# Rows of 320 columns and a chosen byte place for the streamed operands of an encoder's large products

## The chip, the core and the metric

The kernel runs on one core of one Trainium2 chip. The metric is the device time of one execution in microseconds (us). The kernel before takes 2589.96 us, the median of three runs (2589.75 to 2590.74).

A core has a matrix engine (TensorE, PE in the profile), a vector engine (DVE), a scalar engine (ACT), GpSimd (POOL) and a queue engine (SP), which work on a shared on-chip memory (SBUF) of 128 partitions. A matmul multiplies a stationary operand, which a weight load (PEld) brings into the engine, by a streamed operand, whose columns are read one after another from SBUF. The sums land in PSUM.

## What is computed

The reference is a two-layer encoder on 256 tokens with 16 learned tokens ahead of them, 272 positions in all, of width 2048, in float32. Of each layer:

```python
h = rmsnorm(x)
q, k, v, f, ga, gf = split(h @ W_in)            # 2048 -> 6656
a = attention(rope(rmsnorm(q)), rope(rmsnorm(k)), v) @ W_attn_br
s = Re(fft2(f)) @ W_four                        # over positions and 128 channels
x = x + (sigmoid(ga) * a + sigmoid(gf) * s) @ W_out
u = rmsnorm(x) @ W_up                           # 2048 -> 2 * 5632
x = x + (silu(dwconv3(u_gate)) * u_val) @ W_down
```

The 16 learned tokens are dropped at the end, so layer 1 needs only the last 258 positions behind the keys, values and Fourier input, and the last 256 from the gated product on.

## The kernel before, in words

Activations stand transposed: 128 channels on the partitions, positions along the columns. Each float32 value is split in two parts of a rounded type, high and low, and a product takes three matmuls: high weights by high activations, high by low, low by high (lines 246, 247, 248 in `group`). Weights are stationary, 128 by 128 at a time; activations are streamed, 272 columns per matmul in layer 0, 258 or 256 in layer 1. Where twice the width fits 512 columns (layer 1's value half of `W_up` and `W_down`), the first two are one matmul over both parts of the activations (line 242, 512 columns: two rows of 256), followed by line 243 (256 columns).

Weights come as chunks of 512 KB (four contraction tiles by 256 output channels), 864 of them, in a fixed order, on SP's queue into `raw` (four buffers). ACT rounds each into `wh` (line 191), DVE subtracts into `wl` (line 194); `wh` and `wl` have three buffers each, and the split runs up to two chunks ahead of PE. `group` takes its chunks in order: for each contraction tile `kt` (four per chunk) and each of two output tiles `m`, three matmuls. In the last chunk of a group the order is `m` first, then `kt`. So in the other chunks six matmuls in a row read the rows of one `kt`, and in the last chunk three.

The streamed operands of the large products are:

- `xHL`, the normed activations, [16 tiles, high and low, 272 columns]: input projection, gates, `W_up` (groups f, k, v, q, ga, gf, ug, uv)
- `qH`, `qL`, the attention's output, 8 rows each: `W_attn_br` (group a)
- `mH`, `mL`, the gated sum, 8 rows each: `W_out` (group o, twice a layer)
- `gHL`, the feed-forward product, [24, high and low, 272]: `W_down` (group d)

Not among them are the Fourier branch's `fr` (group s, lines 281 and 282), the attention's own operands and the small helper products.

A row of 272 float32 columns is 1088 bytes, four times 256 and 64 more. Tiles stand in SBUF one after another in the order in which they are made. From their sizes follow these places in bytes: `xHL` 33,920; the six buffers of `wh` and `wl` 102,528 and on, each 4,096 long; the per-layer pool from 140,672, in it `mH` 149,376 and `mL` 162,432. Below, the phase of an operand is the place of the first element that a matmul reads, modulo 256. Every 128-column piece of `wh` and `wl` begins at phase 128. The rows of `xHL` begin at phases 128, 192, 0, 64 in turn (high, low, high, low), those of `mH` and of `mL` both at 128, 192, 0, 64 for successive `kt`, and `gHL`'s as `xHL`'s. In layer 1 the streamed part begins 14 columns (56 bytes) or 16 columns (64 bytes) into the row.

Of the kernel before, what the change touches and what calls it, by code (L numbers as in the profile page):

```python
# [10 lines left out]
F32 = mybir.dt.float32  # L11
F32R = mybir.dt.float32r
AF = mybir.ActivationFunctionType
ALU = mybir.AluOpType
# [10 lines left out]
NH = 8  # L25
# [8 lines left out]
MG = 2  # L34
FF_SPLIT = (24, 20)
PRE = 26

def _branch(text):
    return tuple((t[:-1], int(t[-1])) for t in text.split())
# [6 lines left out]
HC = 64  # L46
HC1 = HC + 1
TH = T // 2 + 2
BLK = ((0, 16), (16, 144), (144, 272))

C_COS, C_SIN, C_MASK = 0, T, 2 * T
# [58 lines left out]
def encoder_kernel(ctx, tc, xT, params, consts, bmat, w_in, w_abr, w_four, w_f64, w_out, w_up, w_down, outT):  # L110
# [179 lines left out]
    def first_groups(pss):  # L290
        assert order[st["grp"]][0] == (0, "f01")
        st["grp"] += 1
        ps = [psum.tile([P, 512], F32, tag="mm", name=f"ps_f01_{m}") for m in range(2 * MG)]
        pss += [ps[:MG], ps[MG:]]

        def tile_mm(j, k, h, lo):
            c = k % CW
            for m in range(MG):
                sl = slice(m * P, (m + 1) * P)
                o = ps[MG * j + m][:, :T]  # L300
                a, b = xH[:, k, :], xL[:, k, :]
                nc.tensor.matmul(o, h[:, c, sl], a, start=k == 0, stop=False)
                nc.tensor.matmul(o, h[:, c, sl], b, start=False, stop=False)
                nc.tensor.matmul(o, lo[:, c, sl], a, start=False, stop=k == KT - 1)

        for i, c0, c1, ks in ((0, 0, 1, (0,)), (0, 1, 2, (1,)), (1, 0, 2, ()), (0, 2, 4, (2, 3)), (1, 2, 4, ())):
            for k in ks:
                norm_split(k, P_NM)
            split_w(i, c0, c1, nc.vector if (i, c0) == (0, 0) else None)
        ws = [splits.pop(i) for i in range(2)]  # L310
        st["fetch"] = st["next"] = 2
        for n, (j, k) in enumerate((j, k) for k0 in (0, 2) for j in range(2) for k in (k0, k0 + 1)):
            tile_mm(j, k, *ws[j])
            if n % 2:
                norm_split(CW + n // 2, P_NM)
            if n == 1:
                nc.sync.dma_start(XT[:, 12:16, :], xT[:, 12:16, :])
            if n == 3:
                advance(3)
                pump(len(chunks))  # L320
            step()
        advance(4)
        pump(len(chunks))
        for q in range(1, KT // CW):
            for j in range(2):
                h, lo = splits.pop(st["next"])
                st["next"] += 1
                for c in range(CW):
                    tile_mm(j, CW * q + c, h, lo)
                    if j == 1 and CW * (q + 1) + c < KT:  # L330
                        norm_split(CW * (q + 1) + c, P_NM)
                    if c in (0, 2):
                        advance(st["next"] + (1 if c == 0 else 2))
                        pump(len(chunks))
                    step()


    XT = per.tile([P, KT, T], F32, name="XT")
    xHL = per.tile([P, KT, 2, T], F32R, name="xHL")
    xH, xL = xHL[:, :, 0, :], xHL[:, :, 1, :]  # L340
    prm = per.tile([P, P_N], F32, name="prm")
    cst = per.tile([P, C_N], F32, name="cst")
    ones = per.tile([P, P], F32, name="ones")
    warm = per.tile([P, 1], F32, name="warm")
    mhalf = per.tile([P, 24], F32, name="mhalf")
    BH = per.tile([P, 2, TH], F32R, name="BH")
    BL = per.tile([P, 2, TH], F32R, name="BL")
    bgh = per.tile([P, DEPTH * 2 * KT], F32, name="bgh")
# [33 lines left out]
    nc.gpsimd.memset(remE, 0.0)  # L382
    nc.gpsimd.memset(remO, 0.0)

    cos = cst[:, C_COS:C_COS + T]
    sin = cst[:, C_SIN:C_SIN + T]
    mask = cst[:, C_MASK:C_MASK + T]
# [12 lines left out]

    def norm_split(m, goff):
        gc = prm[:, goff + m:goff + m + 1]
        nc.scalar.activation(xH[:, m, :], XT[:, m, :], AF.Copy, scale=gc)
        nc.vector.scalar_tensor_tensor(xL[:, m, :], XT[:, m, :], gc, xH[:, m, :].bitcast(F32),
                                       op0=ALU.mult, op1=ALU.subtract)

    def norm_sum(m):
        sq = small.tile([P, T], F32, tag="sq", name="sq", bufs=2)
# [32 lines left out]
        nc.vector.tensor_tensor(tok2, tok, tok, op=ALU.mult)  # L441
        holder["tok2"] = tok2

    xr = lambda lo: (lambda kt: (xH[:, kt, lo:T], xL[:, kt, lo:T]))

    for l in range(DEPTH):
        last = l == DEPTH - 1
        lo = 14 if last else 0
        lo2 = 16 if last else 0
        W, W2 = T - lo, T - lo2  # L450
        hold = {}

        with tc.tile_pool(name=f"mix{l}", bufs=1) as mp:
            E = mp.tile([P, NG, T], F32, tag="q1", name="E")
            AHn = 3 * 4 * T
            ALn = 2 * 4 * T
            o1Hf = mp.tile([P, AHn], F32R, tag="aH", name="o1H")
            o1Lf = mp.tile([P, ALn], F32R, tag="aL", name="o1L")
            o1H, o1L = (t_[:, :4 * 4 * HC].rearrange("p (i b c) -> p i b c", i=4, b=4) for t_ in (o1Hf, o1Lf))
            o1r = mp.tile([P, 4, P], F32R, tag="om", name="o1r")  # L460
            fr = mp.tile([P, 4, 2, 2, TH], F32R, name="fr")
            x64 = mp.tile([96, TH], F32R, name="x64")

            def rt(name):
                return mp.tile([P, 2, T], F32, tag="r", name=name, bufs=7)
# [226 lines left out]
            cnt = [0]  # L692
            for pn in pns:
                nc.gpsimd.memset(pn[:, 0:P], 0.0)
            qH = mp.tile([P, NH, T], F32R, tag="q1", name="qH")
            qL = mp.tile([P, NH, T], F32R, tag="q2", name="qL")

            def q_stage(i, qp, qsq):
                kv, j = i // 2, i % 2
# [31 lines left out]
            def attention(kv, rq):  # L731
# [6 lines left out]
                PHf = mp.tile([P, AHn], F32R, tag="aH", name="PH")  # L738
                PLf = mp.tile([P, ALn], F32R, tag="aL", name="PL")
                PH = PHf.rearrange("p (b h t) -> p b h t", b=3, h=4)  # L740
                PL = PLf.rearrange("p (b h t) -> p b h t", b=2, h=4)

                def scores(item):
                    if item is None:
# [102 lines left out]
            for half in range(2):  # L847
                mH = mL = None
                for kind, i in BRANCH_ORDER[half]:
                    j = i - 4 * half  # L850
                    if kind == "ga":
                        tha[i] = gate("ga", i)
                    elif kind == "gf":
                        w64s.append(split_w64(l, i))
                        thf[i] = gate("gf", i)
                    elif kind == "s":
                        def s_evac(m, ps, th=thf[i]):
                            e, o = (mp.tile([P, TH], F32, tag=t, name=t) for t in ("se", "so"))
                            for a, p_ in ((e, ps[0]), (o, ps[1])):
                                nc.scalar.copy(a, p_[:, TH:2 * TH])  # L860
                                nc.vector.tensor_tensor(a, p_[:, :TH], a, op=ALU.add)
                            sp = mp.tile([P, T], F32, tag="sp", name="sp", bufs=2)
                            nc.vector.tensor_tensor(sp[:, 0:TH], e, o, op=ALU.add)
                            nc.vector.tensor_tensor(sp[:, TH:T], e[:, T - TH:0:-1], o[:, T - TH:0:-1], op=ALU.subtract)
                            t_ = th[:, m, lo:T]
                            nc.vector.scalar_tensor_tensor(t_, t_, 1.0, sp[:, lo:T], op0=ALU.add, op1=ALU.mult)

                        four_group((l, "s", i), fr, x64, w64s.pop(0), s_evac)
                    else:
                        if mH is None:  # L870
                            drain()
                            mHf = mp.tile([P, AHn], F32R, tag="aH", name="mH")
                            mLf = mp.tile([P, ALn], F32R, tag="aL", name="mL")
                            mH = mHf[:, :8 * T].rearrange("p (k t) -> p k t", k=8)
                            mL = mLf[:, :8 * T].rearrange("p (k t) -> p k t", k=8)
                        ps = group((l, "a", i), lambda kt: (qH[:, kt, lo:T], qL[:, kt, lo:T]), W)
                        for m in range(MG):
                            k = 2 * j + m
                            t_, h_ = tha[i][:, m, lo:T], mH[:, k, lo:T]
                            nc.vector.scalar_tensor_tensor(t_, t_, 1.0, ps[m][:, :W], op0=ALU.add, op1=ALU.mult)  # L880
                            nc.vector.tensor_tensor(t_, t_, thf[i][:, m, lo:T], op=ALU.add)
                            nc.scalar.copy(h_, t_)
                            nc.vector.tensor_tensor(mL[:, k, lo:T], t_, h_.bitcast(F32), op=ALU.subtract)
                for mg in range(8):
                    ps = group((l, "o", half, mg), lambda kt: (mH[:, kt, lo:T], mL[:, kt, lo:T]), W)
                    for m in range(MG):
                        mt = 2 * mg + m
                        nc.vector.scalar_tensor_tensor(XT[:, mt, lo:T], ps[m][:, :W], 0.5, XT[:, mt, lo:T], op0=ALU.mult, op1=ALU.add)
                        if half == 1:
                            norm_in(mt, P_NF + l * KT)  # L890


        with tc.tile_pool(name=f"ffn{l}", bufs=1) as fp:
# [2 lines left out]
            fused = 2 * W2 <= 512  # L896
            k0 = 0
            for c, n in enumerate(FF_SPLIT):
                gHL = fp.tile([P, FF_SPLIT[0], 2, T], F32R, tag="gHL", name="gHL")
                gH, gL = gHL[:, :, 0, :], gHL[:, :, 1, :]  # L900
                for i in range(k0 // MG, (k0 + n) // MG):
                    ps = group((l, "ug", i), xr(lo), W)
# [2 lines left out]
                    for m in range(MG):  # L905
# [10 lines left out]
                        nc.scalar.activation(cv[:, lo2:T], cv[:, lo2:T], AF.Silu)  # L916
                        nc.vector.tensor_tensor(cv[:, lo2:T], cv[:, lo2:T], rstdB[:, lo2:T], op=ALU.mult)
                        cs.append(cv)
                    ps = group((l, "uv", i), (lambda kt: (xHL[:, kt, :, lo2:T],)) if fused else xr(lo2), W2)
                    for m in range(MG):  # L920
                        j = 2 * i + m - k0
                        cv = cs[m]
# [78 lines left out]
```

## Time and profile before

| | |
|---|---|
| runs | 2589.75, 2589.96, 2590.74 us |
| span of the profiled execution | 2587.5 us, 2.5 us less than the median of the runs |
| PE busy | 2580.3 us, 19,732 matmuls |
| PEld busy | 2517.5 us |
| DVE, ACT, POOL busy | 1691.0, 1211.6, 18.3 us |
| HBM read | 457.35 MB, 178 GB/s over the span |
| granted PE clock | 0.999 of full |

The profile gives for each instruction its start and its time. Matmuls overlap (one is shown for about 0.29 us while the next begins some 0.125 us after it), so what a matmul costs is read from the distance between the starts of two matmuls with a known number between them, not from its shown duration. Starts are printed to 0.01 us.

### The profile page before, as it was taken

Reading aid. Unit: us, or ns where it says so; the run is one execution under the profiler, and the core shown is the slowest. Engines: PE = TensorE matmul, PEld = TensorE weight load, DVE = VectorE, ACT = ScalarE, POOL = GpSimd, SP = SyncE. Lnnn points to the kernel's source line nnn. Section 1 sums busy time; section 2 is a strip of 40 time slices with the busy share of each in tenths; the row PEclk is TensorE's granted clock in tenths of the full one; section 3 lists DMA queues with packets and bytes.
Section 4 is the critical chain, followed back from the end, with each engine's and each line's share of the span. In section 5 each row is a group of like instructions: output and inputs, shape, how many; then the busy total and the mean of one; then the engine's idle time right before and its main releaser. Section 6 shows DMA issues by size and latency. Waiting matters only on the chain.

```text
span 2587.5 us, 47859 instructions
## 1 busy us (share of the span) xinstructions
PE 2580.3 (100%) x19732; PEld 2517.5 (97%) x19732; DVE 1691.0 (65%) x2691; ACT 1211.6 (47%) x1741; POOL 18.3 (1%) x37
## 2 busy tenths in 40 slices
PE   9999999999999999999999999999999999999999
PEld 9999999999999999999999999999999998899988
DVE  7687767766565446565556878677766665566654
ACT  6455434554444334444444555445544543354443
POOL 0000000000000000000000000000000000000000
PEclk9999999999999999999999999999999999999999
DMA  6545655555555555555554546665555555555565
GB/s 234 168 148 164 191 181 188 180 173 177 173 178 172 178 173 177 173 177 174 174 170 151 173 155 199 192 194 188 184 185 186 187 187 187 187 182 186 187 199 159
DMA packets 132011, 465.34 MB, mean 180 GB/s; under 512 B 15312, under 2 KB 19280, under 8 KB 131792
## 3 DMA queue, kind: packets, MB, share of 16 engines
q1 hardware_dynamic: 127424, 457.37, 55.8%
q10 hardware_dynamic: 4368, 4.92, 0.6%
q8 instruction: 154, 2.52, 0.4%
q14 instruction: 65, 0.53, 0.1%
HBM read 457.35 MB, written 2.10 MB: 178 GB/s over the span
## 4 chain that ended last, share of the span: by engine, by line
PE 98%; DVE 1%; ACT 0%; issue 0%; DMA 0%; SPq 0%; DVEq 0%; ACTq 0%
PE ps_ug L247 7%; PE ps_ug L246 7%; PE ps_ug L248 7%; PE ps_uv L242 6%; PE ps_d L242 6%; PE ps_d L246 4%; PE ps_d L247 4%; PE ps_d L248 4%; PE ps_uv L246 3%; PE ps_uv L247 3%; PE ps_uv L248 3%; PE ps_uv L243 3%; PE ps_d L243 3%; PE ps_o L247 2%; PE ps_o L248 2%; PE ps_o L246 2%
## 5 line engine op out<-in xcount | busy, mean ns | idle before, releaser
L194 DVE TENSOR_TENSOR wl<-raw,wh 128x1024 fp32r<-128x1024 f32 (+1 forms) x835 | 1017.1, 1220 | 720.7 <-ACT wh L191 715.6
L191 ACT CAST wh<-raw 128x1024 fp32r<-128x1024 f32 (+1 forms) x834 | 871.2, 1047 | 1025.0 <-issue 166.2
L247 PE MATMUL ps_ug<-xHL,wh 128*128 128x272 f32 (+1 forms) x1408 | 402.4, 286 | 0.0
L246 PE MATMUL ps_ug<-xHL,wh 128*128 128x272 f32 (+1 forms) x1408 | 402.0, 285 | 0.0
L248 PE MATMUL ps_ug<-xHL,wl 128*128 128x272 f32 (+1 forms) x1408 | 401.8, 285 | 0.0
L246 PEld LDWEIGHTS ps_ug<-xHL,wh 128*128 128x128 f32 x1408 | 265.4, 189 | 1.0
L247 PEld LDWEIGHTS ps_ug<-xHL,wh 128*128 128x128 f32 x1408 | 265.5, 189 | 0.1
L248 PEld LDWEIGHTS ps_ug<-xHL,wl 128*128 128x128 f32 x1408 | 265.0, 188 | 0.0
L242 PE MATMUL ps_uv<-xHL,wh 128*128 128x512 f32 x704 | 247.7, 395 | 0.0
L242 PE MATMUL ps_d<-gHL,wh 128*128 128x512 f32 x664 | 233.1, 395 | 0.0
L247 PE MATMUL ps_d<-gHL,wh 128*128 128x272 f32 (+1 forms) x744 | 214.4, 288 | 0.0
L246 PE MATMUL ps_d<-gHL,wh 128*128 128x272 f32 (+1 forms) x744 | 214.1, 288 | 0.0
L248 PE MATMUL ps_d<-gHL,wl 128*128 128x272 f32 (+1 forms) x744 | 214.0, 288 | 0.0
L247 PE MATMUL ps_uv<-xHL,wh 128*128 128x272 f32 x704 | 203.1, 288 | 0.0
L246 PE MATMUL ps_uv<-xHL,wh 128*128 128x272 f32 x704 | 202.9, 288 | 0.0
L248 PE MATMUL ps_uv<-xHL,wl 128*128 128x272 f32 x704 | 202.8, 288 | 0.0
L243 PE MATMUL ps_uv<-xHL,wl 128*128 128x256 f32 x704 | 197.7, 281 | 0.0
L243 PE MATMUL ps_d<-gHL,wl 128*128 128x256 f32 x664 | 186.6, 281 | 0.0
L242 PEld LDWEIGHTS ps_uv<-xHL,wh 128*128 128x128 f32 x704 | 132.4, 188 | 29.8
L242 PEld LDWEIGHTS ps_d<-gHL,wh 128*128 128x128 f32 x664 | 125.0, 188 | 29.2
L246 PE MATMUL ps_ga<-xHL,wh 128*128 128x272 f32 (+1 forms) x512 | 148.1, 289 | 0.0
L246 PE MATMUL ps_gf<-xHL,wh 128*128 128x272 f32 (+1 forms) x512 | 147.1, 287 | 0.0
(284 smaller groups left out, 5906.5 us busy)
## 6 DMA issues: line engine op xcount, KB each, us to landing
raw<-in_w_up SPq DMA_DIRECT2D x352, 512.0 KB, 3.4
raw<-in_w_in SPq DMA_DIRECT2D x207, 512.0 KB, 3.6
raw<-in_w_down SPq DMA_DIRECT2D x176, 512.0 KB, 3.5
raw<-in_w_out SPq DMA_DIRECT2D x64, 512.0 KB, 3.5
raw<-in_w_four SPq DMA_DIRECT2D x32, 512.0 KB, 3.9
raw<-in_w_abr SPq DMA_DIRECT2D x32, 512.0 KB, 3.6
qs<-qp ACTq DMA_DIRECT2D x32, 68.0 KB, 4.0
outT<-ot ACTq DMA_DIRECT2D x16, 128.0 KB, 3.2
```

What stands on the lines that cost most here:

```text
L191: nc.scalar.copy(h[:, a:b], r[:, a:b])
L194: nc.vector.tensor_tensor(lo[:, a:b], r[:, a:b], h[:, a:b].bitcast(F32), op=ALU.subtract)
L242: nc.tensor.matmul(o2, h[:, c, sl], ab, start=kt == 0, stop=False)
L243: nc.tensor.matmul(o, lo[:, c, sl], ab[:, 0, :], start=False, stop=kt == nk - 1)
L246: nc.tensor.matmul(o, h[:, c, sl], a, start=kt == 0, stop=False)
L247: nc.tensor.matmul(o, h[:, c, sl], b, start=False, stop=False)
L248: nc.tensor.matmul(o, lo[:, c, sl], a, start=False, stop=kt == nk - 1)
```

## The change

All four operands get rows of 320 columns (1280 bytes, five times 256), of which a matmul still streams 272, 258 or 256. So all rows of one operand begin at one phase. Where in the row the data begins is given per layer by `X_AT`, `Q_AT` and `G_AT`, in columns. `Q_AT` serves `q` and `m`, `G_AT` serves `g`.

To make room, the scratch at the start of SBUF is cut from 16,384 to 2,048 bytes, and `mL`'s buffer grows to 8 rows of 320. A few tiles are made in another order (`warm` and `mhalf` ahead of `xHL`; `x64`, `E` and `qL` first in the layer's pool; `E`, which shares a buffer with `qH`, has rows of 320 too), which moves the starts.

Worked out from the tiles' sizes, the places after are: `xHL` 19,712 (phase 0); `wh` and `wl` from 94,336 (phase 128, as before); the layer's pool 132,480 (phase 128), in it `qH`, `qL`, `mH`, `mL` all at phase 192, and `gHL` at phase 128. With the offsets the streamed parts begin at

| operand | layer 0 | layer 1 |
|---|---|---|
| `xHL`, full 272 columns | 32 | 96 (groups f, k, v) |
| `xHL`, 258 columns | | 152 |
| `xHL`, 256 columns and pairs | | 160 |
| `q`, `m` | 32 | 152 |
| `gHL` | 32 | 128 |

```diff
+XP = 320
+X_AT, Q_AT, G_AT = (8, 24), (24, 40), (40, 48)
...
-                a, b = xH[:, k, :], xL[:, k, :]
+                a, b = xs(k, 0), xs(k, 1)
...
-    xHL = per.tile([P, KT, 2, T], F32R, name="xHL")
-    xH, xL = xHL[:, :, 0, :], xHL[:, :, 1, :]
+    warm = per.tile([P, 1], F32, name="warm")
+    mhalf = per.tile([P, 24], F32, name="mhalf")
+    xHL = per.tile([P, KT, 2, XP], F32R, name="xHL")
...
+    def xs(k, half, lo=0, l=0):
+        return xHL[:, k, half, X_AT[l] + lo:X_AT[l] + T]
...
-        nc.scalar.activation(xH[:, m, :], XT[:, m, :], AF.Copy, scale=gc)
-        nc.vector.scalar_tensor_tensor(xL[:, m, :], XT[:, m, :], gc, xH[:, m, :].bitcast(F32),
-                                       op0=ALU.mult, op1=ALU.subtract)
+        l = goff // KT % DEPTH
+        h = xs(m, 0, l=l)
+        nc.scalar.activation(h, XT[:, m, :], AF.Copy, scale=gc)
+        nc.vector.scalar_tensor_tensor(xs(m, 1, l=l), XT[:, m, :], gc, h.bitcast(F32), op0=ALU.mult, op1=ALU.subtract)
...
-    xr = lambda lo: (lambda kt: (xH[:, kt, lo:T], xL[:, kt, lo:T]))
+        xr = lambda lo, l=l: (lambda kt: (xs(kt, 0, lo, l), xs(kt, 1, lo, l)))
...
-            E = mp.tile([P, NG, T], F32, tag="q1", name="E")
+            x64 = mp.tile([96, TH], F32R, name="x64")
+            E = mp.tile([P, NH, XP], F32, tag="q1", name="E")[:, :, 0:T]
+            qL = mp.tile([P, NH, XP], F32R, name="qL")[:, :, Q_AT[l]:Q_AT[l] + T]
             AHn = 3 * 4 * T
-            ALn = 2 * 4 * T
+            ALn = 8 * XP
...
-            qH = mp.tile([P, NH, T], F32R, tag="q1", name="qH")
-            qL = mp.tile([P, NH, T], F32R, tag="q2", name="qL")
+            qH = mp.tile([P, NH, XP], F32R, tag="q1", name="qH")[:, :, Q_AT[l]:Q_AT[l] + T]
...
-                            mH = mHf[:, :8 * T].rearrange("p (k t) -> p k t", k=8)
-                            mL = mLf[:, :8 * T].rearrange("p (k t) -> p k t", k=8)
+                            mH, mL = (t_[:, :8 * XP].rearrange("p (k t) -> p k t", k=8)[:, :, Q_AT[l]:Q_AT[l] + T] for t_ in (mHf, mLf))
...
-                gHL = fp.tile([P, FF_SPLIT[0], 2, T], F32R, tag="gHL", name="gHL")
+                gHL = fp.tile([P, FF_SPLIT[0], 2, XP], F32R, tag="gHL", name="gHL")[:, :, :, G_AT[l]:G_AT[l] + T]
...
-                    ps = group((l, "uv", i), (lambda kt: (xHL[:, kt, :, lo2:T],)) if fused else xr(lo2), W2)
+                    ps = group((l, "uv", i), (lambda kt: (xHL[:, kt, :, X_AT[l] + lo2:X_AT[l] + T],)) if fused else xr(lo2), W2)
...
-    nc = _bacc.Bacc("TRN2", target_bir_lowering=False, num_devices=1)
+    nc = _bacc.Bacc("TRN2", target_bir_lowering=False, num_devices=1, dynamic_dma_scratch_size=2048)
```

More of the change, by code (lines that the diff above doesn't have):

```diff
@@ L343, in encoder_kernel @@
     ones = per.tile([P, P], F32, name="ones")
-    warm = per.tile([P, 1], F32, name="warm")
-    mhalf = per.tile([P, 24], F32, name="mhalf")
     BH = per.tile([P, 2, TH], F32R, name="BH")
@@ L461, in encoder_kernel @@
             fr = mp.tile([P, 4, 2, 2, TH], F32R, name="fr")
-            x64 = mp.tile([96, TH], F32R, name="x64")
             def rt(name):
@@ L740, in attention @@
                 PH = PHf.rearrange("p (b h t) -> p b h t", b=3, h=4)
-                PL = PLf.rearrange("p (b h t) -> p b h t", b=2, h=4)
+                PL = PLf[:, :8 * T].rearrange("p (b h t) -> p b h t", b=2, h=4)
                 def scores(item):
```

## The prediction

> **What bounds the kernel now.** I read the page first: the span, the engines' busy time, the chain that ended last, the two weight-split groups.
>
> ```profile
> span 2587.5 us, 47859 instructions
> PE 2580.3 (100%) x19732; PEld 2517.5 (97%) x19732; DVE 1691.0 (65%) x2691; ACT 1211.6 (47%) x1741; POOL 18.3 (1%) x37
> PE 98%; DVE 1%; ACT 0%; issue 0%; DMA 0%; SPq 0%; DVEq 0%; ACTq 0%
> L194 DVE TENSOR_TENSOR wl<-raw,wh 128x1024 fp32r<-128x1024 f32 (+1 forms) x835 | 1017.1, 1220 | 720.7 <-ACT wh L191 715.6
> L191 ACT CAST wh<-raw 128x1024 fp32r<-128x1024 f32 (+1 forms) x834 | 871.2, 1047 | 1025.0 <-issue 166.2
> ```
>
> PE is the bound almost everywhere: 98% of the chain is its own stream of matmuls, 1% (some 26 us) is DVE. So the change is worth what it does to the distance between starts of neighbouring matmuls. DVE and ACT need 1.22 and 1.05 us per chunk of weights; PE takes 3.01 us for it, as the next rows show. These are the first matmuls of the four chunks of one gate group of `W_up` in layer 0 and the first of the next group (timeline of PE: start, duration, line, tiles, shapes); 24 matmuls lie between neighbours.
>
> ```profile
> 701.67 0.29 PE L246 MATMUL ps_ug<-xHL,wh 128*128 128x272 f32 x1
> 704.68 0.29 PE L246 MATMUL ps_ug<-xHL,wh 128*128 128x272 f32 x1
> 707.69 0.29 PE L246 MATMUL ps_ug<-xHL,wh 128*128 128x272 f32 x1
> 710.71 0.29 PE L246 MATMUL ps_ug<-xHL,wh 128*128 128x272 f32 x1
> 713.72 0.29 PE L246 MATMUL ps_uv<-xHL,wh 128*128 128x272 f32 x1
> ```
>
> 12.05 us for 96 matmuls is 125.5 ns for 272 columns. The first three chunks read each `kt`'s rows six times running, the last three times; all take 3.01 or 3.02 us.
>
> Does the place of the operand matter at all? Group o answers it, since `mH` and `mL` stand at one phase for a given `kt`, and the phase moves on by 64 with `kt`. In layer 0 its first chunk has six matmuls at phase 128, six at 192, six at 0, six at 64; here are the first of each six, the first of the second chunk, and the first of the next group, 48 matmuls after the first row:
>
> ```profile
> 353.13 0.29 PE L246 MATMUL ps_o<-mH,wh 128*128 128x272 f32 x1
> 353.89 0.29 PE L246 MATMUL ps_o<-mH,wh 128*128 128x272 f32 x1
> 354.65 0.29 PE L246 MATMUL ps_o<-mH,wh 128*128 128x272 f32 x1
> 355.40 0.28 PE L246 MATMUL ps_o<-mH,wh 128*128 128x272 f32 x1
> 356.14 0.28 PE L246 MATMUL ps_o<-mH,wh 128*128 128x272 f32 x1
> 359.17 0.29 PE L246 MATMUL ps_o<-mH,wh 128*128 128x272 f32 x1
> ```
>
> The sixes take 0.76, 0.76, 0.75 and 0.74 us: 126.7, 126.7, 125.0 and 123.3 ns per matmul, with 6.04/48 = 125.8 for the group (a start is printed to 0.01 us, so a six is known to 1.7 ns per matmul at worst). Same weights' buffers, same width, no wait shown; what differs is the phase. The fast one is 64.
>
> Layer 1, 258 columns, 56 bytes further, so phases 184, 248, 56, 120; rows chosen in the same way:
>
> ```profile
> 1807.16 0.28 PE L246 MATMUL ps_o<-mH,wh 128*128 128x258 f32 x1
> 1807.87 0.28 PE L246 MATMUL ps_o<-mH,wh 128*128 128x258 f32 x1
> 1808.59 0.28 PE L246 MATMUL ps_o<-mH,wh 128*128 128x258 f32 x1
> 1809.31 0.29 PE L246 MATMUL ps_o<-mH,wh 128*128 128x258 f32 x1
> 1810.04 0.28 PE L246 MATMUL ps_o<-mH,wh 128*128 128x258 f32 x1
> 1812.90 0.28 PE L246 MATMUL ps_o<-mH,wh 128*128 128x258 f32 x1
> ```
>
> 0.71, 0.72, 0.72, 0.73 us: 118.3, 120.0, 120.0, 121.7 ns; 5.74/48 = 119.6 for the group. Last the pairs (512 columns, then 256) of `W_down` in layer 1. The first and last row bound a group of 48 pairs. The second to the fourth are two pairs apart: two with rows at phases 192 and 0, then two at 64 and 128.
>
> ```profile
> 2109.49 0.39 PE L242 MATMUL ps_d<-gHL,wh 128*128 128x512 f32 x1
> 2112.28 0.40 PE L242 MATMUL ps_d<-gHL,wh 128*128 128x512 f32 x1
> 2112.99 0.39 PE L242 MATMUL ps_d<-gHL,wh 128*128 128x512 f32 x1
> 2113.68 0.40 PE L242 MATMUL ps_d<-gHL,wh 128*128 128x512 f32 x1
> 2126.34 0.39 PE L242 MATMUL ps_d<-gHL,wh 128*128 128x512 f32 x1
> ```
>
> 16.85/48 = 351.0 ns per pair; 355 at 192 and 0, 345 at 64 and 128.
>
> **The change part by part.** How many matmuls it touches, by operand, each for layer 0 (start of window 0.00) and, for the first, layer 1 (windows view restricted to one tile; PE busy and count):
>
> ```profile
> 0.00:1328.15 1328.15, 863.01 (x6720) 850.21 (x6720) 21.86 (x46) 22.73 (x46) 1.00 0.56 178
> 1328.15:2588.00 1259.85, 819.77 (x6016) 777.39 (x6016) 8.90 (x18) 9.38 (x18) 1.00 0.58 182
> 0.00:1328.15 1328.15, 265.05 (x2110) 265.07 (x2111) 19.28 (x44) 18.35 (x44) 1.00 0.56 178
> 0.00:1328.15 1328.15, 56.29 (x288) 45.65 (x288) 6.35 (x12) 6.17 (x14) 1.00 0.56 178
> 0.00:1328.15 1328.15, 41.37 (x144) 27.11 (x144) 6.35 (x12) 0.60 (x2) 1.00 0.56 178
> 0.00:1328.15 1328.15, 96.96 (x512) 80.65 (x512) 6.28 (x16) 6.16 (x16) 1.00 0.56 178
> 0.00:1328.15 1328.15, 73.97 (x256) 48.19 (x256) 6.28 (x16) 1.00 0.56 178
> ```
>
> These are `xHL` twice, then `gHL`, `qH`, `qL`, `mH`, `mL`. Layer 0 has 6,720 + 2,110 + 288 + 144 + 512 + 256 = 10,030, of which 48 are attention scores with `q` stationary: some 9,980 streams of 272 columns. Of layer 1's 6,016 on `xHL`, 576 (six groups of 96) are 272 wide, 704 pairs make 1,408, and 4,032 are 258 wide; with 1,152 of q and m that is 5,184 of 258. `gHL` adds 664 pairs there (by the loops: 15 fused groups, 8 of 48 pairs and 7 of 40).
>
> Layer 0, all at phase 32. No row has this phase. It is equally far from 0 (125.0) and 64 (123.3), the two cheaper ones of the four. Bounds: the fastest and the slowest six, 123.3 and 126.7, so from -2.2 to +1.2 ns against 125.5. I take the fast end, because it is a neighbour and both slow sixes are 96 or more away: 9,980 x 2.2 = 22.0 us less.
>
> Layer 1, 258 columns at phase 152: midway between 120 (the slowest, 121.7) and 184 (the fastest, 118.3). I take no change; ends -1.3 and +2.1 ns, 5,184 times: -6.7 to +10.9 us. The 576 matmuls at phase 96: no change, ends -1.3 and +0.7 us.
>
> Pairs: on `gHL` both rows at 128, which the fast pairs have for their second row: 345 against 351.0, 664 x 6 = 4.0 us less (other end 664 x 4 = 2.7 more). On `xHL` both at 160, between 128 of the fast pairs and 192 of the slow ones: no change, ends 704 x -6 = -4.2 and 704 x 4 = +2.8 us.
>
> Everything else at nothing. The ACT and DVE writes of `x`, `q`, `m` and `g` keep count, width and order and only land elsewhere; they are covered by PE, with DVE 65% and ACT 47% busy. Were the cover gone, the chunk's 1.22 us would have to reach PE's 3 us first. Next in line when PE gets faster are DVE's waits in the s groups, inside the 26 us above, which do not shrink. The cut scratch: every transfer listed on the page is issued by SP's and ACT's queues, none by POOL's, and the DMA share in the rows above is 0.56; no queue gets an instruction more. The new order of tiles adds no tile and no buffer fewer, so no wait.
>
> Sum: -22.0 - 4.0 = -26.0 us. The profiled execution has 2587.5 us and the median 2.5 us more, which I keep: 2589.96 - 26.0 = 2564 us.
>
> [...]
>
> **The rivals.**
>
> Nothing changes (2590 us). For it: the four chunks above take 3.01 or 3.02 us although the last has another order and so another sequence of phases; a slow six may just be paid back in a fast one, and the mean be set elsewhere. Against it: in group o and in the pairs the sixes differ whenever the phase does, and even rows leave no other phase to pay back from. The Trainium skill, "SBUF — State Buffer", section "SBUF: two separate sides", has PE's ports never waiting on anyone and contention only at the port of DVE and GpSimd; by that rule the place of a stream is free and this rival is the outcome. The sixes speak against it here.
>
> More is won (below 2545 us). All ends on the good side: 22.0 + 1.3 + 6.7 + 4.2 + 4.0 = 38 us. Phases 32 bytes off those seen may be faster than any seen; as much again gives 2590 - 76 = 2514 us. For it: operand and weights would keep one relation for thousands of matmuls, which the trace never shows. Against it: no row shows it.
>
> Slower: the even rows keep the bad relation all the time, where uneven ones visit it a quarter of it. Place: all streams of `group`. Price at the slow ends: 9,980 x 1.2 + 0.7 + 10.9 + 2.7 + 2.8 = 29 us, 2619 us. It decides as soon as layer 0's streams at phase 32 take over 125.5 ns. For it: 152 borders on the slowest phase of 258 columns, 160 on the slow pairs. Against it: 32 lies between the two cheaper phases.
>
> The smaller scratch holds transfers back: PE would wait for `wh`. Against it the queues above.
>
> **How the numbers follow.** Forecast, some gain of the size seen between phases (2545 to 2583 us): 0.45. More won: 0.21. Nothing: 0.09. Slower: 0.22. Scratch: 0.03, slower too. A change under 0.2% (5 us) can hardly be told from none, so the chances are faster 0.66, same 0.09, slower 0.25. The range goes from the doubled gain, 2512, to 2610, short of the worst sum; about a tenth lies beyond on either side. The forecast's own range is 2545 to 2583.
>
> **What would show it.** A gate group of `W_up` in layer 0: 96 matmuls in 11.84 us (123.3 each) instead of 12.05; all sixes of a group o of equal length, 0.74 us in layer 0; 5.74 us for that group in layer 1; neighbours two pairs apart in `W_down` always 0.69 us. Engine counts, DMA and DVE's busy time stay. I am wrong if layer 0's spacing is above 125.5, if it is below 122, if the sixes at one phase still average 125.8, or if PE shows idle time before weights.

## The result, and the profile after

The changed kernel takes 2561.53 us (median of four runs, 2560.89 to 2563.02) against 2589.86 us for the kernel before on the same chip (four runs, 2589.54 to 2590.74): 28.3 us less, a ratio of 0.9892 with a 95% interval of 0.9878 to 0.9906. The forecast was 2564 us.

The page of the kernel after, in the same order as it was read before: span, busy times, chain, the two weight-split groups (their lines are now 196 and 193, and the matmuls of `group` are lines 248 to 250, those of the pairs 244 and 245).

```profile
span 2559.8 us, 47859 instructions
PE 2552.6 (100%) x19732; PEld 2494.2 (97%) x19732; DVE 1690.4 (66%) x2691; ACT 1211.4 (47%) x1741; POOL 18.3 (1%) x37
PE 98%; DVE 1%; DMA 0%; ACT 0%; issue 0%; SPq 0%; DVEq 0%; ACTq 0%
L196 DVE TENSOR_TENSOR wl<-raw,wh 128x1024 fp32r<-128x1024 f32 (+1 forms) x835 | 1016.8, 1220 | 697.3 <-ACT wh L193 692.4
L193 ACT CAST wh<-raw 128x1024 fp32r<-128x1024 f32 (+1 forms) x834 | 871.3, 1047 | 994.4 <-PE ps_ug L249 159.5
```

The counts of instructions are the same on every engine, DVE and ACT work as long as before (1690.4 and 1211.4 us), and PE is still 98% of the chain. The span is 27.7 us shorter, PE's busy time 27.7 us shorter. So all of it lies between the starts of neighbouring matmuls. The same gate group of layer 0 as before (timeline of PE: start, duration, line, tiles, shapes; the first matmul of each of the first four sixes, and the first of the next group, 96 matmuls after the first row):

```profile
693.03 0.28 PE L248 MATMUL ps_ug<-xHL,wh 128*128 128x272 f32 x1
...
693.77 0.28 PE L248 MATMUL ps_ug<-xHL,wh 128*128 128x272 f32 x1
...
694.51 0.28 PE L248 MATMUL ps_ug<-xHL,wh 128*128 128x272 f32 x1
...
695.25 0.28 PE L248 MATMUL ps_ug<-xHL,wh 128*128 128x272 f32 x1
...
704.87 0.28 PE L248 MATMUL ps_uv<-xHL,wh 128*128 128x272 f32 x1
```

Every six takes 0.74 us, and the group 11.84 us, 123.3 ns per matmul. Group o of layer 0, where the sixes had differed with the phase, and below it the first and last row of a group o of layer 1 (48 matmuls of 258 columns, 5.70 us, 118.7 ns each):

```profile
350.40 0.29 PE L248 MATMUL ps_o<-mH,wh 128*128 128x272 f32 x1
...
351.14 0.29 PE L248 MATMUL ps_o<-mH,wh 128*128 128x272 f32 x1
...
351.88 0.29 PE L248 MATMUL ps_o<-mH,wh 128*128 128x272 f32 x1
...
356.32 0.29 PE L248 MATMUL ps_o<-mH,wh 128*128 128x272 f32 x1
...
1632.28 0.28 PE L248 MATMUL ps_o<-mH,wh 128*128 128x258 f32 x1
...
1637.98 0.28 PE L248 MATMUL ps_o<-mH,wh 128*128 128x258 f32 x1
```

The sixes are equal, 0.74 us, and the 48 take 5.92 us. Last the pairs of layer 1: on `xHL` the first of a group of 32 pairs and the first matmul behind it, then on `gHL` the first three pairs of a group of 48 and the first pair behind it.

```profile
1938.87 0.39 PE L244 MATMUL ps_uv<-xHL,wh 128*128 128x512 f32 x1
...
1949.97 0.28 PE L248 MATMUL ps_ug<-xHL,wh 128*128 128x258 f32 x1
...
2085.65 0.39 PE L244 MATMUL ps_d<-gHL,wh 128*128 128x512 f32 x1
...
2085.99 0.40 PE L244 MATMUL ps_d<-gHL,wh 128*128 128x512 f32 x1
...
2086.35 0.39 PE L244 MATMUL ps_d<-gHL,wh 128*128 128x512 f32 x1
...
2102.29 0.39 PE L244 MATMUL ps_d<-gHL,wh 128*128 128x512 f32 x1
```

11.10/32 = 346.9 ns per pair on `xHL`; 16.64/48 = 346.7 on `gHL`. The counterpart on `xHL` before, which the prediction doesn't show:

```profile
1961.84 0.39 PE L242 MATMUL ps_uv<-xHL,wh 128*128 128x512 f32 x1
...
1973.05 0.28 PE L246 MATMUL ps_ug<-xHL,wh 128*128 128x258 f32 x1
```

11.21/32 = 350.3 ns. The table adds, for each kind of group, all distances from one start to the next, after less before. Its means are of the same distances, so they hold the waits inside the groups too.

| group | width | mean ns per matmul before, after | us |
|---|---|---|---|
| layer 0, ug, uv, d | 272 | 125.60, 123.38 | -4.66, -4.69, -4.69 |
| layer 0, o | 272 | 125.82, 123.33 | -1.91 |
| layer 0, gf, ga, a, q, f, k, v | 272 | 128.65, 127.21 | -4.15 |
| layer 1, ug | 258 | 120.19, 120.08 | -0.23 |
| layer 1, gf, ga, o, q, a | 258 | 120.87, 119.91 | -2.96 |
| layer 1, uv (pairs on `xHL`) | 512 + 256 | 350.4, 346.7 per pair | -2.62 |
| layer 1, d (pairs on `gHL`) | 512 + 256 | 351.0, 346.7 per pair | -2.64 |
| layer 1, f, k, v at phase 96 | 272 | 128.02, 128.62 | +0.35 |
| s groups and the rest | | | +0.45 |
| sum | | | -27.75 |

### The profile page after: what moved, and what is told of

Its sections match the earlier page's. It is cut to its first block, busy times and chain, and to the rows that moved or that the text cites. A ratio compares the mean times of both kernels' runs of the same rounds, so it can differ in the third digit from the quotient of the medians.

```text
span 2559.8 us, 47859 instructions
## 1 busy us (share of the span) xinstructions
PE 2552.6 (100%) x19732; PEld 2494.2 (97%) x19732; DVE 1690.4 (66%) x2691; ACT 1211.4 (47%) x1741; POOL 18.3 (1%) x37
## 4 chain that ended last, share of the span: by engine, by line
PE 98%; DVE 1%; DMA 0%; ACT 0%; issue 0%; SPq 0%; DVEq 0%; ACTq 0%
PE ps_ug L249 7%; PE ps_ug L248 7%; PE ps_ug L250 7%; PE ps_uv L244 6%; PE ps_d L244 6%; PE ps_d L249 4%; PE ps_d L250 4%; PE ps_d L248 4%; PE ps_uv L248 3%; PE ps_uv L249 3%; PE ps_uv L250 3%; PE ps_uv L245 3%; PE ps_d L245 3%; PE ps_o L249 2%; PE ps_o L248 2%; PE ps_gf L248 2%
```

## The experiments

The theory: what the place of a stream does depends on its phase against the weights' phase, and the gain comes from having the same good phase in every row. Its rivals: the smaller scratch or the moved tiles do it; any even rows do it, whatever the phase; the streams' own place counts, whatever the weights'. In the tables below a phase is, as before, the first byte read modulo 256. A time without an interval is that of a single run; the granted PE clock is 0.999 or 1.000 in the trace of every kernel here, and spacings are read from the traces.

**The scratch alone.** In the kernel before:

```diff
-    nc = _bacc.Bacc("TRN2", target_bir_lowering=False, num_devices=1)
+    nc = _bacc.Bacc("TRN2", target_bir_lowering=False, num_devices=1, dynamic_dma_scratch_size=2048)
```

> The kernel before with the smaller scratch alone; rows of 272 and all phases as before (the whole layout moves by 14,336 bytes, a multiple of 512). Place theory (the distance between matmul starts hangs on the operand's phase against the weights'): 2590 us, no change within 3 us. Evenness theory (a common phase of all rows is what helps, whichever it is): 2590 us too. Scratch or order theory (the gain comes from the smaller scratch): about 2561 us.

2589.99 us (ten runs) against 2589.32: a ratio of 1.0, interval 0.9991 to 1.001. The cut moves all tiles by 14,336 bytes, which is 56 times 256, and neither it nor the move costs or saves anything that can be measured.

**Other even phases.** Three kernels differ from the changed one in the offsets alone; the added lines are the first, the second and the third.

```diff
-X_AT, Q_AT, G_AT = (8, 24), (24, 40), (40, 48)
+X_AT, Q_AT, G_AT = (0, 0), (32, 48), (0, 0) 
+X_AT, Q_AT, G_AT = (16, 16), (48, 0), (16, 16)
+X_AT, Q_AT, G_AT = (24, 32), (8, 16), (8, 8)
```

> The changed kernel with other offsets, rows still 320 apart. Layer 0: x at phase 0, q and m at 64, g at 128. Layer 1: 258 columns at 56 on x and 184 on m, pairs at 64 on x and 192 on g. Place theory, from the sixes of the trace before: layer 0's groups ug 125.0, o 123.3, d 126.7 ns per matmul; layer 1's ug 120.0, o 118.3; pairs of uv 345, of d 355; in all about 2590 us. Evenness theory: 123.3 in ug, o and d alike, 119.9 and 118.7 in layer 1, pairs 347, as in the changed kernel, about 2561 us.

> As the run before, with layer 0: x at phase 64, q and m at 128, g at 192; layer 1: 258 columns at 120 on x and 248 on m, pairs at 128 on x and 0 on g. Place theory: layer 0's ug 123.3, o 126.7, d 126.7 ns; layer 1's ug 121.7, o 120.0; pairs of uv near 347 as at 128 in the changed kernel's d, pairs of d near 355. Evenness theory: all as in the changed kernel (123.3, 119.9, 118.7, 347).

> Phases that the trace before does not have, layer 0: x at 96, q and m at 224, g at 160; layer 1: 258 columns at 184 on x and 56 on m, pairs at 192 on x and 224 on g. Place theory: values between 122 and 128 ns that differ from group to group in layer 0; layer 1's ug 118.3, o 120.0, pairs of uv 355 and of d about 352. Evenness theory: 123.3 in all of layer 0, 119.9, 118.7, 347.

They took 2598.73, 2575.09 and 2592.59 us, against 2589.32 for the kernel before: even rows are worth anything from 14 us less to 9 us more. The first of them misses both sums, the 2590 us added up from the sixes and the 2561 of evenness alone. The gate group of layer 0 in the first, where `x` stands at 0, first row and the row 96 matmuls later:

```profile
704.99 0.29 PE L248 MATMUL ps_ug<-xHL,wh 128*128 128x272 f32 x1
...
717.15 0.29 PE L248 MATMUL ps_uv<-xHL,wh 128*128 128x272 f32 x1
```

12.16 us, 126.7 ns per matmul: slower than the uneven rows of before, though group o had shown 125.0 for the six at phase 0. A six between sixes at other phases is not what this phase costs when it stands alone. The second kernel, with `x` at 64, shows something else, in group gf of layer 0 (96 matmuls from the first row to the second, and the same for a later group gf):

```profile
258.32 0.34 PE L248 MATMUL ps_gf<-xHL,wh 128*128 128x272 f32 x1
...
270.53 0.29 PE L248 MATMUL ps_a<-qH,wh 128*128 128x272 f32 x1
...
424.75 0.29 PE L248 MATMUL ps_gf<-xHL,wh 128*128 128x272 f32 x1
...
436.59 0.29 PE L283 MATMUL ps_s<-fr,wh 128*128 128x276 f32 x1
```

The same rows of `x` at the same phase, 12.21 us in one group and 11.84 in the other. In three of the eight groups (the third to the fifth) nearly every twelve matmuls took 126.7 ns each, in the last three every twelve took 123.3, with no step between. So one phase can have two steady spacings, and a group stays in the one that it fell into. The first kernel has the same pair of values at 64 in group o of layer 0: 123.3 ns in the first eight groups of 48, 126.7 in the other eight, 125.0 on average.

**The weights moved, the streams not.** A tile of 64 bytes ahead of the weights' buffers moves them from phase 128 to 192; the offsets are set so that every stream keeps the phase that it has in the changed kernel.

```diff
-X_AT, Q_AT, G_AT = (8, 24), (24, 40), (40, 48)
+X_AT, Q_AT, G_AT = (8, 24), (8, 24), (24, 32)
...
+    gap = per.tile([P, 16], F32, name="gap")
+    nc.gpsimd.memset(gap, 0.0)
```

> The changed kernel with the weights' buffers 64 bytes further on (phase 192 instead of 128) and every stream at the phase that it has in the changed kernel. If the relation to the weights counts, a stream at 32 against weights at 192 is as one at 224 against 128: layer 0's ug, uv, o and d near 126.7 ns per matmul (run s3, group o), the pairs of d as at 64 against 128, near 353; total about 2595 us. If the stream's own place counts, whatever the weights' place: 123.3 and 347 as in the changed kernel, 2561 us.

2601.88 us. The gate group of layer 0, and 48 pairs on `gHL` in layer 1:

```profile
706.50 0.29 PE L248 MATMUL ps_ug<-xHL,wh 128*128 128x272 f32 x1
...
718.66 0.29 PE L248 MATMUL ps_uv<-xHL,wh 128*128 128x272 f32 x1
...
2119.53 0.39 PE L244 MATMUL ps_d<-gHL,wh 128*128 128x512 f32 x1
...
2136.49 0.40 PE L244 MATMUL ps_d<-gHL,wh 128*128 128x512 f32 x1
```

12.16/96 = 126.7 ns where the changed kernel has 123.3, and 16.96/48 = 353.3 where it has 346.7, with the streams at the same phases. Where the move brings the distance to the good value it helps: layer 1's groups f, `x` at 96 and weights now at 192, run undisturbed at 123.3 ns where the changed kernel has 125.2 to 126.7. The change's 28 us turn into a loss of 13. The spacing is that of the kernels above in which a stream stands equally far from weights at 128: phase 224 (126.7 ns in the third) and 64 (353.1 ns in the first). The rival that the streams' own place decides is out. A further one is that the writes of ACT and DVE into the weights' buffers, which move too, disturb the streams. Taking the distances in ug, uv, d and o of layer 0 apart by what those engines do at the time, they are 126.7 ns while both work, while DVE alone is idle and while ACT alone is idle, and 123.3 in the changed kernel in all three cases; so the writes aren't what sets the spacing.

What fits is that PE's own two reads, of weights and of stream, bear on each other. The Trainium skill, "SBUF — State Buffer", section "SBUF: two separate sides", says that PE's port waits on no other user of the memory, and no rule there covers two reads by PE itself. What this run shows is that the two places matter together; that the reads themselves collide is inferred.

**The distance changed by 256 bytes.** Two pad tiles, before `xHL` and ahead of the weights, put `xHL` 256 and the weights 512 bytes further; `x` stands at 64, as in the second kernel above.

```diff
-X_AT, Q_AT, G_AT = (8, 24), (24, 40), (40, 48)
+X_AT, Q_AT, G_AT = (16, 16), (40, 24), (32, 32)
...
+    pads = [per.tile([P, 64], F32, name="pad0")]
...
+    pads.append(per.tile([P, 64], F32, name="pad1"))
+    for pad in pads:
+        nc.gpsimd.memset(pad, 0.0)
```

> As run s2 for x (phase 64 in layer 0; 120 and pairs at 128 in layer 1), but xHL begins 256 bytes further on, the weights 512 further on, so that high and low rows of x have swapped their places modulo 512. If 256 bytes is the whole period: ug 123.3, layer 1's ug 119.1, pairs of uv 352 as in s2. If the period is 512 bytes: ug about 126.7 (group o, which alternates between the two, had 125.0 at 64, and ug 123.3), pairs of uv about 347 as the pairs of d in the changed kernel. q and m at 96 and g at 0 in layer 0, m at 88 and pairs of d at 64 in layer 1 are new points: with a period of 256, o 125.9, d 126.7, pairs of d 353.

2578.54 us. A gate group of layer 0, its first matmul and the one 96 later:

```profile
695.48 0.28 PE L248 MATMUL ps_ug<-xHL,wh 128*128 128x272 f32 x1
...
707.32 0.28 PE L248 MATMUL ps_uv<-xHL,wh 128*128 128x272 f32 x1
```

With `x` at 64, 11.84/96 = 123.3 ns as in the second kernel; layer 1's gate groups with `x` at 120 have 119.1 ns in both. 256 bytes of distance change nothing there, and 128 do (64 gives 123.3, 192 gives 126.7, below), so, as far as these places show, the relation counts modulo 256. Group o's 125.0, which the expectation set against this, was the average of two spacings. The pairs on `xHL`, at 128 in both kernels, begin at 346.7 to 346.9 ns (one group of 32 pairs in the second kernel, three here) and then stand at 353.0; behind the first d groups the same happens again, after two groups. So 128 has two spacings for pairs as well. The total is 3.4 us above the second kernel's, though groups o and d of layer 0 have 125.3 and 126.7 ns in both: most of it is in layer 1, in the pairs on `gHL` (353.3 ns at 64 against 351.1 at 0, 1.4 us), in group o (120.0 ns at 88 against 118.9 at 248, 0.9 us) and in the s groups (0.8 us).

**Uneven rows again.** The changed kernel with rows 64 bytes longer, so that they begin at four phases in turn, as before.

```diff
-XP = 320
+XP = 336
```

> The changed kernel with rows 336 columns apart (five times 256 bytes and 64 more), so that successive rows begin at four phases again, 32, 96, 160 and 224 in layer 0. Place theory: layer 0's groups at the mean of what the even rows gave at these phases (123.3, 125.9, 125.7, 126.7): about 125.4 ns, so about 2590 us in all. Evenness alone gives no other number here; if unequal rows cost something of their own, layer 0 lies above 126 ns.

2587.3 us against 2589.23: of the 28 us only about 2 are left. The gate group, in which the phases 32, 96, 160 and 224 take turns:

```profile
702.39 0.29 PE L248 MATMUL ps_ug<-xHL,wh 128*128 128x272 f32 x1
...
714.46 0.29 PE L248 MATMUL ps_uv<-xHL,wh 128*128 128x272 f32 x1
```

12.07/96 = 125.7 ns, near the old 125.5. The start at 32, the order of the tiles and the scratch are all those of the changed kernel, so it takes the even rows as well as the good phase.

**Finer places.** Offsets that are no multiple of 32 bytes, and later a second set (the second added line) that was to tell whether multiples of 8 bytes matter.

```diff
-X_AT, Q_AT, G_AT = (8, 24), (24, 40), (40, 48)
+X_AT, Q_AT, G_AT = (9, 40), (26, 8), (44, 24)
+X_AT, Q_AT, G_AT = (11, 24), (30, 9), (47, 48) 
```

> The changed kernel with fine steps about phase 32 in layer 0: x at 36, q and m at 40, g at 48; layer 1: 258 columns at 216 on x and 24 on m, pairs at 224 on x and 32 on g. If the place counts in lines of 32 bytes or more: 123.3 ns in ug, o and d still; if single columns count, they differ from it by a ns or more. Layer 1 gives new points, between 118 and 122 ns and between 345 and 355.

> The changed kernel with other fine steps: layer 0 x at 44, q and m at 56, g at 60; layer 1 m at 28; the rest as it was. Run s4 had 126.7 at 36, but 123.3 at 40 and 48. If what costs is a start that is no multiple of 8 bytes: 126.7 in ug (44) and d (60), 123.3 in o (56), and layer 1's o above 118.7 (28). If 36 was only a bad place in a 256-byte pattern: 44 between 40 and 48 should be near 123.3.

2582.0 and 2564.14 us. In the first, layer 0 has `x` at 36 and `m` at 40, four bytes apart (a group o of 48, then a gate group of 96):

```profile
355.02 0.28 PE L248 MATMUL ps_o<-mH,wh 128*128 128x272 f32 x1
...
360.94 0.28 PE L248 MATMUL ps_o<-mH,wh 128*128 128x272 f32 x1
...
703.95 0.29 PE L248 MATMUL ps_ug<-xHL,wh 128*128 128x272 f32 x1
...
716.11 0.29 PE L248 MATMUL ps_uv<-xHL,wh 128*128 128x272 f32 x1
```

5.92/48 = 123.3 ns at 40 and 12.16/96 = 126.7 at 36: one column decides 3.3 ns, the whole distance between the good and the bad value. In the second kernel 44 gave 123.3, 60 gave 123.3 and 56 gave 126.7 ns. 44 and 60 are no multiples of 8 and fast, 56 is one and slow, so that idea fell.

**Weights and streams moved together by four bytes.** The buffers of `wh` and `wl` get 64 columns more and are used from the second column on (weights at 132); all streams move by four bytes too, but for the pairs on `gHL`, which go to 36.

```diff
-X_AT, Q_AT, G_AT = (8, 24), (24, 40), (40, 48)
+X_AT, Q_AT, G_AT = (9, 25), (25, 41), (41, 25)
...
-            splits[i] = tuple(wp.tile([P, CW, MG * P], F32R, tag=t, name=f"{t}{i}") for t in ("wh", "wl"))
+            splits[i] = tuple(wp.tile([P, CW * MG * P + 64], F32R, tag=t, name=f"{t}{i}")[:, 1:1 + CW * MG * P]
+                              .rearrange("p (c n) -> p c n", c=CW) for t in ("wh", "wl"))
```

> Weights and streams of the changed kernel all begin one column (4 bytes) later: weights at 132, layer 0's streams at 36, layer 1's at 156, 164 and, on g, 36 (in run s4 pairs of d at 32 took 346.7). Run s4 had 126.7 ns in layer 0's ug with x at 36 against weights at 128. If the relation alone counts, down to one column: 123.3 in all of layer 0's groups and 346.7 for the pairs, 2561 us. If a stream's own place counts at that grain: 126.7 in layer 0, about 2591 us.

2621.29 us, the slowest of all. A gate group of layer 0, its first matmul and the one 96 later:

```profile
715.29 0.29 PE L249 MATMUL ps_ug<-xHL,wh 128*128 128x272 f32 x1
...
727.61 0.29 PE L249 MATMUL ps_uv<-xHL,wh 128*128 128x272 f32 x1
```

12.32/96 = 128.3 ns, slower than any phase with weights at 128 or 192, and the pairs on `xHL` take 360.0. So the relation modulo 256 is not the whole rule: at this grain it also counts where weights and stream start themselves. Nor is it a loss everywhere: layer 1's gate groups of 258 columns take 119.0 ns where the changed kernel has 120.0. Since weights at 132 were tried only with the streams moved along, and no other small offset was, it stays open which of the two starts counts, and at which grain.

**The best values together.** With each operand at the best phase found so far: everything in layer 0 at 32, 258 columns at 24, all pairs at 32.

```diff
-X_AT, Q_AT, G_AT = (8, 24), (24, 40), (40, 48)
+X_AT, Q_AT, G_AT = (40, 24), (24, 8), (40, 24)
...
+    pads = [per.tile([P, 32], F32, name="pad0")]
...
+    pads.append(per.tile([P, 32], F32, name="pad1"))
+    for pad in pads:
+        nc.gpsimd.memset(pad, 0.0)
```

> The best phases found, put together: layer 0 all at 32 as in the changed kernel; layer 1's 258 columns at 24 on x, q and m, its pairs at 32 on x and g (xHL begins 128 bytes further on, the weights 256). Place theory, from m at 24 in run s4 (117.8 ns against 118.7): a and o give 1.0 us; x's 4,032 streams of 258 columns, if they come to 117.8 too, 6 to 8 us; pairs as in the changed kernel (346.7); six groups of layer 1 at 224 cost 0.4 us. In all 2553 to 2560 us. If x at 24 behaves as x at 152 (119.9 in ug), 2561 us.

2563.53 us (four runs), a ratio of 0.990 to the kernel before, interval 0.9885 to 0.9915, which overlaps that of the changed kernel: no better, and above the 2553 to 2560 us hoped for. A group o and a gate group of layer 1 (48 and 96 matmuls), both with streams of 258 columns at 24:

```profile
1632.60 0.28 PE L248 MATMUL ps_o<-mH,wh 128*128 128x258 f32 x1
...
1638.25 0.28 PE L248 MATMUL ps_o<-mH,wh 128*128 128x258 f32 x1
...
1926.78 0.28 PE L248 MATMUL ps_ug<-xHL,wh 128*128 128x258 f32 x1
...
1938.41 0.39 PE L244 MATMUL ps_uv<-xHL,wh 128*128 128x512 f32 x1
```

117.7 ns in group o, 121.1 in the gate group. The first gate group still runs stretches at 117.8; from the second on each twelve matmuls take 121.1 or 121.2, to the last one. So the best and the worst spacing of 258 columns stand at one phase, and even on the same rows of `x`. What came before probably decides; no run shows it.

**The changed kernel once more**, beside the last one, to see whether it repeats itself.

> The changed kernel once more, beside the run before it on the same chip: 2561 us, layer 0's groups at 123.3 ns.

2561.34 us (four runs, 2560.86 to 2563.32), ratio 0.9894, interval 0.9877 to 0.991. The same group o of layer 1 as in the result:

```profile
1631.92 0.28 PE L248 MATMUL ps_o<-mH,wh 128*128 128x258 f32 x1
...
1637.68 0.28 PE L248 MATMUL ps_o<-mH,wh 128*128 128x258 f32 x1
```

5.76 us where the other execution of the same program had 5.70: even one kernel falls into one spacing or another at phase 152. It costs little here, since 48 matmuls differ by 0.06 us and eight such groups did so.

Put together, the spacings of undisturbed stretches of twelve matmuls (four pairs) with weights at phase 128, or at 192 brought to the same relation, over all kernels with even rows but the one with weights at 132:

| phase | 272 columns, ns | pair, ns | | phase | 258 columns, ns |
|---|---|---|---|---|---|
| 0 | 126.7 | 350 to 352 | | 24 | 117.8 or 121.2 |
| 32 | 123.3 | 346.7 | | 28 | 118.3 |
| 36 | 126.7 | | | 56 | 120.0 |
| 40, 44, 48, 60 | 123.3 | | | 88 | 120.0 |
| 56 | 126.7 | | | 120 | 118.8 to 120.0 |
| 64 | 123.3 or 126.7 | 353 | | 152 | 118 to 120.0 |
| 96 | 125.0 to 126.7 | 353 | | 184 | 119.0 to 120.5 |
| 128 | 125.0 to 126 | 346.7 or 351 to 355 | | 216 | 118.7 to 119.7 |
| 160 | 125.0 to 126 | 346.7 | | 248 | 118 or 120.0 |
| 192 | 126.7 | 351 to 354 | | | |
| 224 | 125.3 or 126.7 | 350 | | | |

At 32 in layer 0, over the three kernels with it there, 2,240 of 2,442 stretches of twelve were within 0.25 ns of 123.5, and none was at 126.7.

## Why the prediction was right, and where not

**Layer 0 at phase 32, -22.0 us: right in size, half right in reason.** 123.33 ns was measured for 123.3, and the groups gave -20.1 us. The missing 1.9 us are in gf, ga, a, q, f, k and v: their undisturbed stretches gained what was forecast (in gf from 125.6 to 123.3 ns), but these groups also hold waits, and the waits grew. By estimate they are 9 us before and 11 after: the mean distances of the table less 125.5 and 123.3, times 2,880 matmuls. The reason given was that 32 is a neighbour of two cheap phases, 0 and 64. The first of the even kernels shows 126.7 at 0, so one of the two was not cheap at all; and 36 at 126.7 shows that a value can't be carried even four bytes. The row was read as the price of a phase; it was the price of a passage through it. Taking the fast end was lucky to that extent: of the eight multiples of 32, layer 0's streams are faster than before at 32 always, at 64 mostly, and at the six others their undisturbed stretches stand between 125.0 and 126.7, about level or slower.

**258 columns at 152, no change: -3.2 us**, inside the ends of -6.7 and +10.9. The gate groups, 2,112 of the matmuls, indeed kept their 120.0 ns or so (120.06 before, 119.99 after); the other groups found a faster spacing. That another execution of the same kernel differs in group o says that this term isn't fixed by the place alone.

**Pairs on `gHL`, -4.0 us: -2.64.** They run at 346.7 ns and not at 345. The 345 came from 0.69 us over two pairs, and a start printed to 0.01 us leaves room for 346.7. That even this came was luck in part: 128 is the place at which the pairs on `xHL` of two other kernels went over from 346.7 to 353.0 ns, which would have been a loss of 1.3 us (an estimate: 664 pairs by 2.0 ns more than before). **Pairs on `xHL`, no change: -2.62 us.** Phase 160 gives the same 346.7, which the neighbours, fast and slow, could not tell.

**576 matmuls at 96, no change: +0.35 us.** **Everything else at nothing:** held. DVE and ACT keep their busy times, the scratch has a ratio of 1.0 (0.9991 to 1.001), and the s groups, whose waits were named as next in line, together with the rest got 0.45 us longer.

Against the forecast sum of -26.0 the trace has -27.75: +1.9 in layer 0, +1.3 in the pairs on `gHL`, -2.6 in those on `xHL`, -3.2 in the 258 columns, +0.8 in the rest. The medians differ by another 0.6 us, less than the four runs of the changed kernel differ among themselves (2.1 us). The measured signs were those stated: 11.84 us for a gate group, 0.74 for all sixes, 0.69 or 0.70 for two pairs; only group o of layer 1 was 5.70 rather than 5.74.

**The rivals.** That nothing changes because a slow six is paid back elsewhere has a true core: with uneven rows the mean came to 125.5 and 125.7 for the two sets of four phases that were run, the kernel before and the one with 336 columns. Even rows take that averaging away, and the outcome then is that of the one phase left, or one of its two. The slower rival was a live one: the even kernels with `x` at 0 and with the weights moved by 64 bytes lose 9 and 13 us, at the price named (126.7 ns in layer 0), though not at phase 32. More than 38 us was found by no kernel.

**What stays open.** Why the spacings are these few values, why one column can cost 3.3 ns, and what decides at entry between two spacings. That the spacing hangs on the places of weights and stream together is shown by moving the one and not the other; that their reads collide is inferred, and by what mechanism was not measured. The Trainium skill, "TensorE: Matmul & The Clock Gate", section "Back-to-back issue gap", would put 272 columns at 115.8 ns (an estimate) by its formula for an isolated matmul, which it sets apart from a stream that loads weights for each. No run here reached it; the best steady spacing is 123.3 ns.

## What to carry to other kernels

Where PE runs back to back and loads weights for every matmul, the byte place of the streamed rows against the weights' is worth measuring: here it is 1.1% of the time, and more than that was lost by a tile of 64 bytes put ahead of the weights. Give all rows one phase modulo 256 first, then try several phases on the chip, since a value can't be inferred from neighbours or from a row that shares its group with other phases. Afterwards keep tiles' sizes and order fixed, because a new tile ahead can undo it. Pads of 256 bytes, where they were tried, left layer 0's gate groups at 123.3 ns.

## What was not expected

- Two steady spacings at one place: 126.7 and 123.3 ns in groups gf at phase 64; 346.7 and 353.0 ns for pairs at phase 128; 117.8 and 121.2 ns for 258 columns at phase 24. They last over whole groups.
- Four bytes count: 126.7 ns at 36 against 123.3 at 32 and 40, and 128.3 with weights and streams both moved by four bytes.
- A tile of 64 bytes that PE never reads costs 40 us (2561.5 to 2601.9), by moving the weights while all streams keep their phases.
